# A decoder block on one core: the first loads, the first norm and the constants' addresses are rearranged

## The chip, the core and the metric

The kernel is one program on one of the eight cores of a Trainium2 chip. A core has five engines, each with an instruction stream of its own: TensorE (PE; its weight loads are shown apart as PEld) multiplies matrices, VectorE (DVE), ScalarE (ACT) and GpSimd (POOL) work element by element, and SyncE (SP) issues DMAs. An engine takes its instructions strictly in order; where one waits on a semaphore, all behind it wait too. Data lies in SBUF (128 partitions), results of TensorE in PSUM, everything else in HBM, from which 16 DMA engines load.

The metric is the device time of one execution in microseconds (us); less is better.

## What is computed

One layer of a decoder at 1024 tokens and width 1024, in float32: RMSNorm, an input projection for two kinds of attention with a learned bias by distance, an output projection, a gated feed-forward part, and a final RMSNorm. Cut to what matters here:

```python
h = rmsnorm(x, g_attn[l])
proj = h @ w_in[l]
qa, ka, va, qb, kb, vb = jnp.split(proj, 6, axis=-1)
oa = dilated_attention(qa, ka, va, bias_dil)            # bias from rel_bias by log bucket of distance
lam = (jnp.exp(jnp.sum(lq[0] * lq[1])) - jnp.exp(jnp.sum(lq[2] * lq[3])) + lam_init)
ob = diff_attention(qb, kb, vb, bias_diff, lam, subln_g[l], lam_init)
x = x + jnp.concatenate([oa, ob], axis=-1) @ w_out[l]
h = rmsnorm(x, g_ffn[l])
gate, up = jnp.split(h @ w_gate_up[l], 2, axis=-1)
x = x + (jax.nn.silu(gate) * up) @ w_down[l]
return rmsnorm(x, g_final)
```

with `rmsnorm(x, g) = x * rsqrt(mean(x * x) + eps) * g`.

## The kernel before

All matrix operands are kept as a high part (float32 rounded to the format that TensorE multiplies fast) and a low part (what the rounding left), and each product is the sum of three: high by high, high by low, low by high. The high part is a cast on ScalarE, the low part a subtraction on VectorE or GpSimd.

The first stage, up to about 51 us, is what the change touches. The 1024 tokens are eight tiles of 128. For each tile t the kernel loads `xt_t` (512 KB), squares and sums it on ScalarE (L159), works out `r = (mean + eps) ** -0.5` (`rms_power`, L139 ff.), multiplies by r and by `ga`, the norm's weights, into `hn_a` (two halves on VectorE, L167), transposes that with TensorE against the identity `ident` (`tp_a`, L178, two groups of four), copies the transposes to `hTh` (ScalarE, L181) and what is left to `hTl` (VectorE, L182). Between the tiles TensorE runs `project_v` (L223): the values of two differential heads, 24 matmuls a tile into `vpsd`, against two weight tiles of 512 KB, `w_vd00` and `w_vd01`. Those are loaded as `raw_vd`, cast by ScalarE (L136) and subtracted (L137) by GpSimd for the first and by VectorE for the second. Behind the eight tiles come the query and key weights and projections (`raw_qd`, `raw_kd`, `w_qd`, `ppsqd`).

`rms_power` has two forms. Without `pool` the power is a Ln and an Exp on ScalarE and three small operations on VectorE that refine the result (L148 to L152). With `pool` it is one power on GpSimd (L145). Before, the norm at the start ("a") uses the first form, the norm ahead of the feed-forward part ("f") and the last norm the second.

Beside that, the stage makes the table of biases: `rb` (the learned table) and `hot` (one-hot buckets by distance) are multiplied by TensorE into three PSUM tiles `gps` (L349), VectorE adds `mask` to each and writes `gt` (L350), which is stored as `gtab` (L351) for the attention to read in strips. The lambda of the differential attention comes from `lq` (L364) in two products `lo` on VectorE (L371) and an Exp on ScalarE.

All DMAs are issued from SP's queue, in the order of the code's calls as far as the scheduler keeps it; eight completion semaphores are used in turn, so a DMA is issued only when the one eight places ahead has landed. On the other engines a scheduler orders the instructions from its own estimate of the times, so an edit can move rows that it doesn't name. The tile pools are stacks: those on the left begin behind the constants, those on the right end at the top of SBUF.

The order of the first loads is that of these lines:

```python
    load_x(0)
    nc.sync.dma_start(hot, maps[:N_BUCKETS, :])
    nc.sync.dma_start(rb, rel_bias)
    nc.sync.dma_start(ga, broadcast(g_attn[0], D))
    nc.sync.dma_start(mask, maps[N_BUCKETS:, :])
    nc.sync.dma_start(ident, eye)
```

Of the kernel before, what the change touches and what calls it, by code (L numbers as in the profile page):

```python
# [12 lines left out]
F32 = mybir.dt.float32  # L13
F32R = mybir.dt.float32r
AF = mybir.ActivationFunctionType
ALU = mybir.AluOpType
# [3 lines left out]
P = 128  # L20
S = 1024
D = 1024
# [4 lines left out]
N_HEADS = N_DIL + N_DIFF  # L27
D_FF = 2816
NFF = D_FF // P
N_BUCKETS = 32  # L30
# [4 lines left out]
EPS = 1e-6  # L35
# [5 lines left out]
POOL_POWER = "f"  # L41
# [30 lines left out]
def tile_hybrid_block(  # L72
# [17 lines left out]
    nc = tc.nc  # L90
    mm = nc.tensor.matmul

    cp = ctx.enter_context(tc.tile_pool(name="const", bufs=1))
# [9 lines left out]
    def psum(tag, name):  # L103
        return pp.tile([P, 512], F32, tag=tag, bufs=BANKS[tag], name=name)
# [2 lines left out]
        return ap.partition_broadcast(P) if ap.shape == [n] else ap  # L107


    ident = cp.tile([P, P], F32, name="ident")  # L110
    ones = cp.tile([P, P], F32R, name="ones")
    nhalf = cp.tile([P, 1], F32, name="nhalf")
# [6 lines left out]
    def broadcast(ap1d, n):  # L119
        return bass.AP(tensor=ap1d.tensor, offset=ap1d.offset, ap=[[0, P], [1, n]])  # L120


    def split_weights(src, a, name, tag="w", eng=None, parts=None):

        small = tag == "w"
        pool = wp if small else mapp
        raw = pool.tile([P, 1024], F32, tag="raw" if small else "KL", bufs=1 if small else 2, name=f"raw_{name}")
        nc.sync.dma_start(raw.rearrange("p (a b) -> p a b", a=a), src)
        if parts:
            w = parts  # L130
        elif small:
            w = [pool.tile([P, 1024], F32R, tag=tag, bufs=4, name=f"w_{name}_{i}") for i in "hl"]
        else:
            both = pool.tile([P, 2, 1024], F32R, tag=tag, name=f"w_{name}")
            w = [both[:, i, :] for i in range(2)]
        nc.scalar.copy(w[0], raw)  # L136
        (eng or nc.gpsimd).tensor_tensor(w[1], raw, w[0].bitcast(F32), op=ALU.subtract)  # L137
        return [w_.rearrange("p (a b) -> p a b", a=a) for w_ in w]

    def rms_power(st, eps, pool=False):  # L140

        m, r = st[:, 0:1], st[:, 1:2]
        nc.vector.tensor_scalar(m, m, 1.0 / D, eps, op0=ALU.mult, op1=ALU.add)  # L143
        if pool:
            nc.gpsimd.tensor_tensor(r, m, nhalf, op=ALU.pow)  # L145
            return
        u = st[:, 2:3]
        nc.scalar.activation(r, m, AF.Ln)  # L148
        nc.scalar.activation(r, r, AF.Exp, scale=-0.5)
        nc.vector.scalar_tensor_tensor(u, r, m, r, op0=ALU.mult, op1=ALU.mult)  # L150
        nc.vector.tensor_scalar(u, u, -0.5, 1.5, op0=ALU.mult, op1=ALU.add)
        nc.vector.tensor_tensor(r, r, u, op=ALU.mult)  # L152

    def norm(pool, src, g_b, t, name, hn=None):

        st = pool.tile([P, 3], F32, tag="nst", name=f"nst_{name}{t}")
        if hn is None:
            hn = pool.tile([P, D], F32, tag="hn", bufs=3 if name == "a" else LAG, name=f"hn_{name}{t}")
        nc.scalar.activation(hn, src, AF.Square, accum_out=st[:, 0:1])  # L159
        rms_power(st, EPS, name in POOL_POWER)  # L160
        for half in range(2):
            cols = slice(half * 512, (half + 1) * 512)
            if half and f"{name}{t}" in SHARED:
                nc.scalar.mul(hn[:, cols], src[:, cols], st[:, 1:2])
                nc.gpsimd.tensor_tensor(hn[:, cols], hn[:, cols], g_b[:, cols], op=ALU.mult)
                continue
            nc.vector.scalar_tensor_tensor(  # L167
                hn[:, cols], src[:, cols], st[:, 1:2], g_b[:, cols], op0=ALU.mult, op1=ALU.mult
            )
        return hn  # L170

    def transpose_in(hn, th, tl, t, name):

        for half in range(2):
            ps = psum("T", f"tp_{name}{t}_{half}")
            for i in range(4):
                k = 4 * half + i
                nc.tensor.transpose(ps[:, i * P : (i + 1) * P], hn[:, k * P : (k + 1) * P], ident)  # L178
            pv = ps.rearrange("p (a b) -> p a b", a=4)
            dst = (slice(None), slice(4 * half, 4 * half + 4), slice(t * P, (t + 1) * P))  # L180
            nc.scalar.copy(th[dst], pv)  # L181
            nc.vector.tensor_tensor(tl[dst], pv, th[dst].bitcast(F32), op=ALU.subtract)  # L182
# [14 lines left out]
    gtab = dp.tile([N_HEADS, GLEN], F32, name="gtab")  # L197
# [122 lines left out]
    def load_x(t):  # L320
        xts[t] = sp.tile([P, D], F32, tag="xt", bufs=3, name=f"xt_{t}")
        nc.sync.dma_start(xts[t], x[0, t * P : (t + 1) * P, :])

    rb = sp.tile([N_BUCKETS, N_HEADS], F32, tag="rb", bufs=1, name="rb")
    load_x(0)
    hot = sp.tile([N_BUCKETS, GLEN], F32, tag="hot", bufs=1, name="hot")
    nc.sync.dma_start(hot, maps[:N_BUCKETS, :])
    nc.sync.dma_start(rb, rel_bias)
    mask = sp.tile([N_HEADS, GLEN], F32, tag="mask", bufs=1, name="mask")
    ga = sp.tile([P, D], F32, tag="ga", bufs=1, name="ga")  # L330
    nc.sync.dma_start(ga, broadcast(g_attn[0], D))
    nc.sync.dma_start(mask, maps[N_BUCKETS:, :])
    nc.sync.dma_start(ident, eye)
    ones_f = sp.tile([P, P], F32, tag="ones_f", bufs=1, name="ones_f")
    nc.vector.memset(ones_f, 1.0)
    nc.vector.tensor_copy(ones, ones_f)
    vd = []
    wv = [
        split_weights(
            w_in_v[:, 4 * i : 4 * i + 4, VB : VB + 256], 4, f"vd0{i}", ("QS", "KH")[i], nc.vector if i else None  # L340
        )
        for i in range(2)
    ]

    gt = sp.tile([N_HEADS, GLEN], F32, tag="gt", bufs=1, name="gt")
    for c in range(3):
        ps = psum("S", f"gps_{c}")
        cols = slice(c * 384, (c + 1) * 384)
        mm(ps[:N_HEADS, :384], rb, hot[:, cols], start=True, stop=True)  # L349
        nc.vector.tensor_tensor(gt[:, cols], ps[:N_HEADS, :384], mask[:, cols], op=ALU.add)  # L350
    nc.sync.dma_start(gtab, gt)  # L351
    gen_vd = project_v(VB, False, "d0", vd, wv)
    for t in range(KT):
        if t == 0:
            load_x(1)
        if t + 2 < KT:
            load_x(t + 2)
        transpose_in(norm(sp, xts[t], ga, t, "a"), hTh, hTl, t, "a")
        if t > 0:
            next(gen_vd)  # L360
# [464 lines left out]
    def block_tile(p, up):  # L825
        return mxp.tile([P, 4, 512], F32, tag="mix", name=f"{('gate', 'act')[up]}_{p}")
# [68 lines left out]
    with tc.manual_schedule(engines={mybir.EngineType.PE, mybir.EngineType.Pool}):  # L895
        for i, t in enumerate(TOKENS):
            for n in range(2):
                out_proj_group(mix, wo[n], t, n, "l")
            high = xp.tile([P, D], F32, tag="x1t", name=f"hn_f{t}") if t % 2 else None
            hns[t] = norm(mid, x1[t], gf, t, "f", high)  # L900
            nc.sync.dma_start(x1_d[t], x1[t])
            if 2 <= i < 6:
                flip_low(i - 2)
            if i >= 3 and i < 7:
                split(raw0[0][i - 3], a0[0][i - 3], nc.gpsimd)
        for i in range(4):
            split(raw0[1][i], a0[1][i], nc.gpsimd)
# [29 lines left out]
    for p in range(1, NPAIR):  # L937
        for up in range(2):
# [3 lines left out]
            c = block_tile(p, up)  # L942
# [16 lines left out]
    def next_bank(name):  # L959
        n_ps[0] += 1  # L960
        return psum(CYCLE[n_ps[0] % 8], name)
# [37 lines left out]
    for c0 in range(0, NPAIR - 1, 2):  # L999
# [3 lines left out]
        for i in ORDER:  # L1003
# [14 lines left out]
            for tq in range(4):  # L1018
                ps = next_bank(f"d{c0}_{i}_{tq}")
# [29 lines left out]
    for m, rows in ((0, (2, 3)), (1, (4, 5))):  # L1049
        for tq in range(4):  # L1050
            sl = slice(tq * P, (tq + 1) * P)
            t = 2 * tq + m
            y = xp.tile([P, D], F32, tag="x1t", name=f"y_{t}")
            st = dn.tile([P, 2], F32, tag="fst", bufs=8, name=f"fst_{t}")
            junk = mxp.tile([P, D], F32, tag="mix", name=f"sq_{t}")
            halves = t == KT - 1
            for n, r in enumerate(rows):
                ps = next_bank(f"dl_{t}_{n}")
                i = 0
                for k in range(2):  # L1060
                    a, w = oal[2 * m + k], wl[2 * k + n]
# [3 lines left out]
                cols = slice(n * 512, (n + 1) * 512)  # L1065
# [8 lines left out]
            for n in range(2):  # L1074
                cols = slice(n * 512, (n + 1) * 512)
# [30 lines left out]
```

## Time and profile before

| | |
|---|---|
| median of three runs | 1250.87 us (1249.38 to 1251.2) |
| the profiled execution | 1254.24 us |
| its span, first to last instruction | 1252.5 us |
| mean granted TensorE clock | 0.99 |
| first transposes start | 11.13 us |
| first matmul of the query projection | 51.38 us |

How to read the profile: a row of the timeline has start, duration, engine, source line, operation, the tile written <- the tiles read, the shapes, how many instructions were merged, and in brackets how long the engine was idle just before and what released it. Rows of several instructions run from the first one's start to the last one's end. A row of stretches has, for each engine, the time busy and the number of instructions, then the granted TensorE clock (1.00 is full), the share of time in which the DMA engines were busy, and GB/s. A row of a group has its count, then busy time and the mean duration in ns, then the idle time ahead of it. A row of DMA issues has how many, KB each, and the median time from issue to landing. In the page's slices each digit is a tenth of one of 40 equal slices.

### The profile page before, as it was taken

To read this page: it belongs to the slowest core of one execution; us is meant where nothing else is said; L and a number is where in the kernel's file an instruction comes from. 1 tells how busy PE (TensorE), PEld (TensorE's weight loads), DVE (VectorE), ACT (ScalarE), POOL (GpSimd) and SP (SyncE) were. 2 spreads that over 40 slices of the span, in tenths; PEclk is the share of its full clock that TensorE was granted. 3 is DMA by queue.
4 is the path that set the end of the run, shared out by engine and by line. 5 is a ranking of instruction groups with operands and counts; after the bars stand their busy time and mean duration, and the time that the engine had idled before them with its cause. 6 is when DMAs were issued, how large, how long until landed. Compare 5 with 4: busy or idle time off the path is not lost. (4 is left out here: it accounts for less than half of the span.)

```text
span 1252.5 us, 18470 instructions
## 1 busy us (share of the span) xinstructions
PE 1219.6 (97%) x6318; PEld 1040.9 (83%) x6318; DVE 785.4 (63%) x1667; ACT 576.4 (46%) x1300; POOL 737.3 (59%) x664
## 2 busy tenths in 40 slices
PE   6999999999999999998999999999999999999996
PEld 5989989988998888876788888888888887888885
DVE  6548688876766587858554455554545535655597
ACT  5346567665765565535433443434343433222214
POOL 2024344354443443426936797889878786956676
PEclk8999999999999999998999999999999999999999
DMA  6232233132213383252232345333544369966633
GB/s 217 67 89 71 62 98 89 42 93 87 83 51 108 118 307 132 85 173 104 84 121 88 145 169 184 135 120 133 185 168 175 129 244 372 403 230 253 220 126 134
DMA packets 99613, 184.63 MB, mean 147 GB/s; under 512 B 6920, under 2 KB 58376, under 8 KB 99520
## 3 DMA queue, kind: packets, MB, share of 16 engines
q1 hardware_dynamic: 99520, 183.46, 41.9%
q8 instruction: 50, 0.82, 0.3%
q14 instruction: 43, 0.35, 0.1%
HBM read 119.41 MB, written 55.63 MB: 140 GB/s over the span
## 5 line engine op out<-in xcount | busy, mean ns | idle before, releaser
L1024 PE MATMUL d<-wd,oa 128*128 128x512 f32 x840 | 192.9, 391 | 2.8 <-DMA oa<-act_d 2.6
L1024 PEld LDWEIGHTS d<-wd,oa 128*128 128x128 f32 x840 | 158.5, 189 | 36.9 <-ACT acc L1027 3.0
L1029 DVE TENSOR_TENSOR acc<-d,acc 128x512 f32<-128x512 f32 x128 | 86.5, 687 | 62.7 <-PE d L1024 56.6
L547 POOL TENSOR_SCALAR t_a<-t_a,st_a 128x384 f32<-128x384 f32 (+2 forms) x96 | 55.3, 586 | 104.7 <-DVE st_a L443 71.7
L691 ACT CAST wd<-raw_d 128x512 fp32r<-128x512 f32 x74 | 45.1, 622 | 141.7 <-PE d L1024 95.3
L692 POOL TENSOR_TENSOR wd<-raw_d,wd 128x512 fp32r<-128x512 f32 x54 | 73.0, 1372 | 60.6 <-ACT wd L691 60.6
L692 POOL TENSOR_TENSOR ao<-act,ao 128x512 fp32r<-128x512 f32 x52 | 75.3, 1457 | 42.2 <-ACT ao L691 41.8
L692 POOL TENSOR_TENSOR wu<-raw_u,wu 128x512 fp32r<-128x512 f32 x50 | 69.5, 1408 | 29.8 <-ACT wu L691 17.1
L691 ACT CAST wg<-raw_g 128x512 fp32r<-128x512 f32 x70 | 42.2, 620 | 88.8 <-POOL raw_g L705 43.3
L692 POOL TENSOR_TENSOR wg<-raw_g,wg 128x512 fp32r<-128x512 f32 x50 | 75.0, 1517 | 3.2 <-DVE act L797 2.0
L691 ACT CAST wu<-raw_u 128x512 fp32r<-128x512 f32 x70 | 40.6, 619 | 70.7 <-DMA raw_u<-in_w_gate_up 28.4
L433 ACT ACTIVATE t_d<-t_d,st_d 128x384 f32<-128x384 f32 (+3 forms) x96 | 58.5, 612 | 14.4 <-DVE st_d L420 13.9
L433 ACT ACTIVATE t_a<-t_a,st_a 128x384 f32<-128x384 f32 (+2 forms) x96 | 58.7, 613 | 12.6 <-DVE st_a L420 11.9
L458 ACT CAST ath_a<-tp_a 128x384 fp32r<-128x384 f32 (+2 forms) x96 | 45.1, 478 | 41.4 <-PE tp_a L452 40.3
L752 PE MATMUL pc_g<-h,wg 128*128 128x512 f32 x240 | 59.4, 390 | 0.0
L752 PE MATMUL pa_u<-h,wu 128*128 128x512 f32 x240 | 59.3, 392 | 0.0
L752 PE MATMUL pc_u<-h,wu 128*128 128x512 f32 x240 | 59.2, 389 | 0.0
L752 PE MATMUL pa_g<-h,wg 128*128 128x512 f32 x240 | 58.7, 390 | 0.3 <-ACT gate L778 0.3
L752 PE MATMUL pd_u<-h,wu 128*128 128x512 f32 x240 | 58.5, 389 | 0.0
L752 PE MATMUL pd_g<-h,wg 128*128 128x512 f32 x240 | 57.8, 390 | 0.0
L505 POOL TENSOR_SCALAR t_d<-t_d,st_d 128x384 f32<-128x384 f32 (+3 forms) x48 | 30.1, 637 | 46.8 <-DVE st_d L443 32.2
L691 ACT CAST ao<-act 128x512 fp32r<-128x512 f32 x74 | 42.4, 619 | 32.2 <-DVE act L765 12.2
(275 smaller groups left out, 3577.7 us busy)
## 6 DMA issues: line engine op xcount, KB each, us to landing
act_d<-ao SPq DMA_DIRECT2D x74, 512.0 KB, 3.3
oa<-act_d SPq DMA_DIRECT2D x74, 512.0 KB, 4.9
raw_g<-in_w_gate_up SPq DMA_DIRECT2D x11, 1024.0 KB, 5.7
raw_u<-in_w_gate_up SPq DMA_DIRECT2D x11, 1024.0 KB, 6.2
raw_d<-in_w_down SPq DMA_DIRECT2D x11, 1024.0 KB, 10.1
strip<-gtab SPq DMA_DIRECT2D x12, 512.0 KB, 3.7
xt<-in_x SPq DMA_DIRECT2D x8, 512.0 KB, 5.0
raw_o<-in_w_out SPq DMA_DIRECT2D x8, 512.0 KB, 3.8
```

The costliest lines, as they stand in the source:

```text
L433: nc.scalar.activation(tt[:, :n], tt[:, :n], AF.Exp, bias=st[:, last : last + 1], scale=-1.0, accum_out=st[:, 2 + c : 3 + c],)
L458: nc.scalar.copy(hi, pv)
L505: nc.gpsimd.tensor_scalar(t0[:, :n], t0[:, :n], s0[:, 4:5], 1.0, op0=ALU.mult, op1=ALU.mult)
L547: nc.gpsimd.tensor_scalar(t0[:, :n], t0[:, :n], s0[:, 4:5], 1.0, op0=ALU.mult, op1=ALU.mult)
L691: nc.scalar.copy(dst[:, 0], src)
L692: eng.tensor_tensor(dst[:, 1], src, dst[:, 0].bitcast(F32), op=ALU.subtract)
L752: mm(ps, a[:, l_, k, :], b[:, r_, k, :], start=start and i == 0, stop=i == 11, skip_group_check=not start,)
L1024: mm(ps, a[:, l_, sl], w[:, r_, :], start=n == 0, stop=n == 5)
L1029: v.tensor_tensor(acc[i][:, tq], ps, acc[i][:, tq], op=ALU.add)
```

## The change

Five edits, four of them in the first stage.

- `rb`, `hot`, `ident` and `mask` are loaded from ScalarE's queue, ahead of its first square.
- SP's queue begins with x's first tile, the first weight, `ga`, x's second tile and the second weight.
- The additions of `mask` to `gps` are written as a function that is called ahead of the fourth token tile; the three matmuls keep their place, with three PSUM tiles taken at once.
- The first two token tiles take their power from GpSimd.
- A pad of 128 bytes is put ahead of `ident`. `ident` and `ones` then start at a multiple of 256 bytes (before: 128 past one), and every tile of the left-hand pools moves from a multiple of 256 to 128 past it. The right-hand pools stay.

```diff
+    cp.tile([P, 32], F32, name="const_pad")
     ident = cp.tile([P, P], F32, name="ident")
...
-        rms_power(st, EPS, name in POOL_POWER)
+        rms_power(st, EPS, name in POOL_POWER or name == "a" and t < 2)
...
-    load_x(0)
     hot = sp.tile([N_BUCKETS, GLEN], F32, tag="hot", bufs=1, name="hot")
-    nc.sync.dma_start(hot, maps[:N_BUCKETS, :])
-    nc.sync.dma_start(rb, rel_bias)
     mask = sp.tile([N_HEADS, GLEN], F32, tag="mask", bufs=1, name="mask")
     ga = sp.tile([P, D], F32, tag="ga", bufs=1, name="ga")
-    nc.sync.dma_start(ga, broadcast(g_attn[0], D))
-    nc.sync.dma_start(mask, maps[N_BUCKETS:, :])
-    nc.sync.dma_start(ident, eye)
+    load_x(0)
+    for dst, src in ((rb, rel_bias), (hot, maps[:N_BUCKETS, :]), (ident, eye), (mask, maps[N_BUCKETS:, :])):
+        nc.scalar.dma_start(dst, src)
...
-    wv = [
-        split_weights(
+
+    def first_weights(i):
+        return split_weights(
             w_in_v[:, 4 * i : 4 * i + 4, VB : VB + 256], 4, f"vd0{i}", ("QS", "KH")[i], nc.vector if i else None
         )
-        for i in range(2)
-    ]
+
+    wv = [first_weights(0)]
+    nc.sync.dma_start(ga, broadcast(g_attn[0], D))
+    load_x(1)
+    wv.append(first_weights(1))
...
+    g_ps = [psum("S", f"gps_{c}") for c in range(3)]
     for c in range(3):
-        ps = psum("S", f"gps_{c}")
-        cols = slice(c * 384, (c + 1) * 384)
-        mm(ps[:N_HEADS, :384], rb, hot[:, cols], start=True, stop=True)
-        nc.vector.tensor_tensor(gt[:, cols], ps[:N_HEADS, :384], mask[:, cols], op=ALU.add)
-    nc.sync.dma_start(gtab, gt)
+        mm(g_ps[c][:N_HEADS, :384], rb, hot[:, c * 384 : (c + 1) * 384], start=True, stop=True)
+
+    def bias_tables():
+        for c in range(3):
+            cols = slice(c * 384, (c + 1) * 384)
+            nc.vector.tensor_tensor(gt[:, cols], g_ps[c][:N_HEADS, :384], mask[:, cols], op=ALU.add)
+        nc.sync.dma_start(gtab, gt)
+
     gen_vd = project_v(VB, False, "d0", vd, wv)
     for t in range(KT):
-        if t == 0:
-            load_x(1)
         if t + 2 < KT:
             load_x(t + 2)
+        if t == 3:
+            bias_tables()
         transpose_in(norm(sp, xts[t], ga, t, "a"), hTh, hTl, t, "a")
```

The scheduler makes the following of it. First SP's queue, from the program's start; a name's first number is the token tile or the weight's half, the last one only counts buffers. Before:

```order
L322 DMA xt_0_111<-in_x 128x1024
L327 DMA hot_113<-in_maps 32x1152
L328 DMA rb_110<-in_rel_bias 32x12
L331 DMA ga_117<-in_g_attn 128x1024
L332 DMA mask_116<-in_maps 12x1152
L333 DMA ident_71<-in_eye 128x128
L128 DMA raw_vd00_124<-in_w_in 128x4x256
L128 DMA raw_vd01_129<-in_w_in 128x4x256
L322 DMA xt_1_145<-in_x 128x1024
```

And now, ScalarE's queue behind SP's:

```order
L323 DMA xt_0_115<-in_x 128x1024
L129 DMA raw_vd00_124<-in_w_in 128x4x256
L343 DMA ga_114<-in_g_attn 128x1024
L323 DMA xt_1_130<-in_x 128x1024
L129 DMA raw_vd01_132<-in_w_in 128x4x256
L323 DMA xt_2_144<-in_x 128x1024
L370 DMA lq_586<-in_lambda_qk 128x256
L371 DMA gsub_78<-in_subln_g 128x1
L129 DMA raw_qd0_605<-in_w_in 128x8x128
```

```order
L331 DMA rb_111<-in_rel_bias 32x12
L331 DMA hot_112<-in_maps 32x1152
L331 DMA ident_72<-in_eye 128x128
L331 DMA mask_113<-in_maps 12x1152
L160 ACTIVATE hn_a0_147,nst_a0_146<-xt_0_115 128x1024
L137 CAST w_vd00_126<-raw_vd00_124 128x1024
L160 ACTIVATE hn_a1_170,nst_a1_169<-xt_1_130 128x1024
L137 CAST w_vd01_134<-raw_vd01_132 128x1024
L182 CAST hTh_89<-tp_a0_0_153 128x4x128
```

The first weight stands ahead of `ga` and x's second tile ahead of the second weight; on ScalarE the second tile's square has moved ahead of the second weight's cast, and both are ahead of the first tile's copies.

VectorE, from its first norm on (`nst` holds mean and r, `lo` and `lst` are the lambda's products). Before:

```order
L350 TENSOR_TENSOR gt_134<-gps_0_135,mask_116 12x384
L151 TENSOR_SCALAR nst_a0_149<-nst_a0_149 128x1
L152 TENSOR_TENSOR nst_a0_149<-nst_a0_149 128x1
L167 SCALAR_TENSOR_TENSOR hn_a0_150<-xt_0_111,nst_a0_149,ga_117 128x512 x2
L350 TENSOR_TENSOR gt_134<-gps_1_138,mask_116 12x384
L350 TENSOR_TENSOR gt_134<-gps_2_141,mask_116 12x384
L137 TENSOR_TENSOR w_vd01_131<-raw_vd01_129,w_vd01_131 128x1024
L182 TENSOR_TENSOR hTl_89<-tp_a0_0_160,hTh_88 128x4x128
L182 TENSOR_TENSOR hTl_89<-tp_a0_1_167,hTh_88 128x4x128
```

And now:

```order
L168 SCALAR_TENSOR_TENSOR hn_a0_147<-xt_0_115,nst_a0_146,ga_114 128x512 x2
L355 TENSOR_TENSOR gt_137<-gps_0_138,mask_113 12x384
L355 TENSOR_TENSOR gt_137<-gps_1_139,mask_113 12x384
L355 TENSOR_TENSOR gt_137<-gps_2_140,mask_113 12x384
L144 TENSOR_SCALAR nst_a1_169<-nst_a1_169 128x1
L168 SCALAR_TENSOR_TENSOR hn_a1_170<-xt_1_130,nst_a1_169,ga_114 128x512 x2
L138 TENSOR_TENSOR w_vd01_134<-raw_vd01_132,w_vd01_134 128x1024
L183 TENSOR_TENSOR hTl_90<-tp_a0_0_153,hTh_89 128x4x128
L377 ISA lo_0_591,lst_590<-lq_586 128x64
L377 ISA lst_590 128x1
```

Four more small rows of the lambda follow (`gsub`, `lo_1`, `lst`), and then the other low half of tile 0. The table's sums stand together behind the first tile's product, and the second tile's product has moved from behind the low parts of tile 0 to ahead of the second weight's subtraction.

TensorE, from the projection of tile 0's last terms on. Before:

```order
L223 MATMUL vpsd0_0_203<-w_vd01_131,hTh_88 128x256 x4
L178 MATMUL tp_a1_0_187<-ident_71,hn_a1_177 128x128 x4
L178 MATMUL tp_a1_1_194<-ident_71,hn_a1_177 128x128 x4
L223 MATMUL vpsd0_1_259<-w_vd00_126,hTh_88 128x256 x2
L178 MATMUL tp_a2_0_245<-ident_71,hn_a2_235 128x128 x4
L223 MATMUL vpsd0_1_259<-w_vd00_126,hTl_89 128x256
```

And now (`vpsd0_0` is tile 0's product, and these are its last 16 matmuls and what stands between them):

```order
L179 MATMUL tp_a1_0_176<-ident_72,hn_a1_170 128x128 x4
L224 MATMUL vpsd0_0_192<-w_vd00_126,hTl_90 128x256 x4
L179 MATMUL tp_a1_1_183<-ident_72,hn_a1_170 128x128 x4
L224 MATMUL vpsd0_0_192<-w_vd01_134,hTl_90 128x256 x4
L224 MATMUL vpsd0_0_192<-w_vd00_126,hTh_89 128x256 x4
L224 MATMUL vpsd0_0_192<-w_vd01_134,hTh_89 128x256 x4
L224 MATMUL vpsd0_1_248<-w_vd00_126,hTh_89 128x256 x2
```

Tile 1's transposes have moved into tile 0's product, and tile 2's, which stood inside tile 1's, now stand behind it. On GpSimd the two powers stand one ahead of and one behind the first weight's subtraction. Behind this stage TensorE's and SP's rows are as before; in the second norm, between 560 and 600 us, the scheduler swapped a few rows on VectorE, ScalarE and GpSimd.

## The prediction

> **What bounds the kernel now.** I read the page first, for the engine that is never free and for the slices in which it is.
>
> ```profile
> span 1252.5 us, 18470 instructions
> PE 1219.6 (97%) x6318; PEld 1040.9 (83%) x6318; DVE 785.4 (63%) x1667; ACT 576.4 (46%) x1300; POOL 737.3 (59%) x664
> PE   6999999999999999998999999999999999999996
> PEclk8999999999999999998999999999999999999999
> ```
>
> TensorE is busy 97% of the span; the 33 us in which it is not lie mostly in the first and the last of the 40 slices (31 us each). Every part of the change but the pad lies in the first. So the second view is that stage in stretches:
>
> ```profile
> core 0: us, PE busy (x) PEld busy (x) DVE busy (x) ACT busy (x) POOL busy (x), PEclk, DMA share, GB/s
> 0.00:11.10 11.10, 3.99 (x6) 0.66 (x6) 2.44 (x11) 3.35 (x6) 0.19 (x4) 1.00 0.79 250
> 15.56:18.97 3.41, 3.16 (x15) 3.16 (x16) 3.21 (x18) 2.17 (x8) 0.54 (x1) 1.00 0.12 47
> 18.97:22.38 3.41, 1.47 (x11) 1.02 (x10) 3.38 (x4) 1.27 (x3) 1.81 (x1) 1.00 0.02 1
> 22.38:29.20 6.82, 6.15 (x28) 5.93 (x29) 5.49 (x14) 5.20 (x15) 1.55 (x1) 0.50 0.75 240
> 29.20:51.40 22.20, 22.20 (x191) 22.19 (x191) 17.41 (x46) 11.63 (x34) 0.84 (x1) 1.00 0.35 111
> ```
>
> Until 11.1 us TensorE has only the bias table. From 18.97 to 22.38 it works 1.47 of 3.41 us, and in the 6.8 us after that its granted clock is 0.50. From 29.2 us it is full to the stage's end, the first matmul of the next stage:
>
> ```profile
> 11.13 1.94 PE L178 MATMUL tp_a<-ident,hn_a 128*128 128x128 f32 x8 [1.24 <-DVE hn_a L167]
> 13.48 2.08 PE L223 MATMUL vpsd<-w_vd,hTh 128*128 128x256 f32 x8 [0.41 <-ACT hTh L181]
> 17.68 1.69 PE L223 MATMUL vpsd<-w_vd,hTh 128*128 128x256 f32 x8
> 21.48 0.63 PE L178 MATMUL tp_a<-ident,hn_a 128*128 128x128 f32 x4 [1.68 <-DVE nst_a L152]
> 23.05 0.79 PE L223 MATMUL vpsd<-w_vd,hTh 128*128 128x256 f32 x2 [0.93 <-ACT hTh L181]
> 51.38 0.40 PE L250 MATMUL ppsqd<-hTh,w_qd_h 128*128 128x512 f32 x1
> ```
>
> So the measure is the start of token tile 1's projection, 23.05 us: what stands behind it on TensorE (168 projections, 48 transposes) is the same before and after, and what it gains is kept through the full stages behind, unless TensorE waits anew. What holds it back is on ScalarE, VectorE and GpSimd:
>
> ```profile
> 5.07 1.06 ACT L159 ACTIVATE hn_a<-xt 128x1024 f32<-128x1024 f32 x1 [3.07 <-DMA xt<-in_x]
> 10.59 1.05 ACT L136 CAST w_vd<-raw_vd 128x1024 fp32r<-128x1024 f32 x1 [3.72 <-DMA raw_vd<-in_w_in]
> 11.90 1.05 ACT L136 CAST w_vd<-raw_vd 128x1024 fp32r<-128x1024 f32 x1 [0.26 <-DMA raw_vd<-in_w_in]
> 12.85 1.06 ACT L181 CAST hTh<-tp_a 128x512 fp32r<-128x512 f32 x2
> 9.45 0.55 DVE L350 TENSOR_TENSOR gt<-gps,mask 12x384 f32<-12x384 f32 x1 [2.32 <-DMA mask<-in_maps]
> 10.28 1.42 DVE L167 SCALAR_TENSOR_TENSOR hn_a<-xt,nst_a,ga 128x512 f32<-128x512 f32 x2
> 12.98 2.18 DVE L137 TENSOR_TENSOR w_vd<-raw_vd,w_vd 128x1024 fp32r<-128x1024 f32 x1 [0.36 <-ACT w_vd L136]
> 15.08 1.28 DVE L182 TENSOR_TENSOR hTl<-tp_a,hTh 128x512 fp32r<-128x512 f32 x2
> 17.79 3.55 DVE L167 SCALAR_TENSOR_TENSOR hn_a<-xt,nst_a,ga 128x512 f32<-128x512 f32 x2
> 21.44 1.41 DVE L167 SCALAR_TENSOR_TENSOR hn_a<-xt,nst_a,ga 128x512 f32<-128x512 f32 x2
> 11.72 2.35 POOL L137 TENSOR_TENSOR w_vd<-raw_vd,w_vd 128x1024 fp32r<-128x1024 f32 x1 [11.29 <-ACT w_vd L136]
> 18.43 2.35 POOL L137 TENSOR_TENSOR w_qd_l<-raw_qd,w_qd_h 128x1024 fp32r<-128x1024 f32 x1 [4.36 <-ACT w_qd_h L136]
> ```
>
> Two things are to be seen. The first transposes are done by about 13 us, but their copies (12.85) stand behind the second weight's cast (11.90). And a VectorE operation that reads two SBUF tiles stops while GpSimd subtracts: token 1's pair takes 3.55 us, token 2's 1.41; its second half ends 0.5 us behind GpSimd's 18.43 + 2.35 = 20.78. The weight's subtract, 2.18 us, ends 15.16, 1.09 us after GpSimd's at 14.07: held for 1.09 of it.
>
> **Loads.** Issue to landing, and the small ones:
>
> ```profile
> ga<-in_g_attn SPq DMA_DIRECT2D x1, 512.0 KB, 7.0
> 2.09 0.42 SPq L331 DMA_DIRECT2D ga<-in_g_attn  x1
> 5.91 3.99 PE L349 MATMUL gps<-hot,rb 32*12 32x384 f32 x6 [5.91 <-DMA rb<-in_rel_bias]
> 3.40:6.80 3.40, 0.90 (x2) 0.26 (x3) 0.15 (x1) 1.48 (x4) 0.00 (x0) 1.00 0.76 235
> hot<-in_maps SPq DMA_DIRECT2D x1, 144.0 KB, 4.4
> ```
>
> The two weights land 11.90 - 10.59 = 1.31 us apart, the pace of 512 KB. ga landed at 2.09 + 7.0 = 9.09, 3.2 us behind rb (5.91), with the engines 76% busy: 2.4 us of transfer (bounds 1.31 and 3.2). The four small loads, 264 KB, are 0.67 us at that pace whichever queue issues them. Now xt0 lands at 5.07, the first weight at 5.07 + 1.31 + 0.67 = 7.05, ga at 9.45, xt1 at 10.76, the second weight at 12.07 (it was 11.90), xt2 at 13.4, lq and gsub at 13.7, the query weight at 15.0. Putting the weights ahead of ga is paid back by x's second tile ahead of the second weight: it gains nothing (bounds 10.3 and 12.9). If the small loads took nothing from the big ones, the second weight would land at 11.4. [...] ScalarE's four issues, at SP's 0.42 us, fill a wait of 3.07 us and cost nothing; without that wait they would cost 1.7.
>
> **The engines, step by step.** GpSimd's power costs 0.55 us in the last stage, and takes from VectorE three small operations a token and from ScalarE two:
>
> ```profile
> 1247.53 0.55 POOL L145 TENSOR_TENSOR fst<-fst,nhalf 128x1 f32<-128x1 f32 x1 [0.35 <-DVE fst L143]
> L150 DVE SCALAR_TENSOR_TENSOR nst_a<-nst_a 128x1 f32<-128x1 f32 x8 | 3.3, 410 | 0.5 <-ACT nst_a L149 0.5
> L148 ACT ACTIVATE nst_a<-nst_a 128x1 f32<-128x1 f32 x8 | 1.7, 207 | 0.7 <-DVE nst_a L143 0.7
> ```
>
> - Token 0: squares end 6.25, power 7.0; ga is there at 9.45, but GpSimd subtracts from the first weight's cast (7.05 + 1.05 = 8.1) to 10.45 and holds the pair: 10.45 to 11.9 (it was 10.28).
> - The three table sums stand right behind it, though written for the fourth tile: 1.5 us (0.5 each), to 13.4. Their 2.32 us wait for the mask is gone, but it kept nobody: hn_a waited for ga.
> - Token 1: mean 13.5, power 14.1, pair to 15.5 (it was 21.3: six us earlier). The weight's subtract, not held, 1.09: 16.6. The first half of token 0's low part 0.64: 17.25.
> - ScalarE: square of token 1 10.76 to 12.0; second weight 12.07 to 13.1; token 0's copies to 14.2 (it was 13.9); square of token 2 to 15.4; query weight to 16.45. So GpSimd subtracts from 16.45 to 18.8.
> - VectorE's next is lo, the lambda product, which reads two SBUF tiles. **I take it as held** until 18.8: then 0.5 us of small work and the other low half, to 19.9 (it was 16.36).
> - TensorE needs that for the last 12 matmuls of token 0: at half clock 0.21 each (8 in 1.69, above), 2.5 us: **22.4**, against 23.05, so 0.65 earlier. ScalarE's copy of token 1 (behind the lambda's Exp 19.5, the square of token 3 20.7 and one Ln) ends at 21.5 and keeps nobody.
>
> Given back: token 2's transposes stood inside token 1's projection and now stand behind it, so token 2's projection waits for copy and low part, 0.57 + 0.64, less the second four transposes (0.6) and two matmuls: 0.4 us (0 to 0.9). Sum: -0.65 + 0.4 = **-0.25 us**. The small operations that VectorE no longer does lie beside that wait and are in the times above.
>
> Whether lo is held is not in the trace: the bounds are 0 and 2.35 us, and the nearest rows, pair and weight, were held. [...]
>
> **The pad** sets the identity and the ones at 256 bytes, and moves all tiles of the left-hand pools from 0 to 128 past such a boundary. The trace has no such tile under full load; its nearest rows are xt (64 past), whose loads ran at the pace above, and the transposes' operand hn_a (128 past). I take 0. Should it cost DMA time, the price is bounded by TensorE's later waits for DMAs, doubled: 2.6 + 1.4 us; a gain can't exceed them either.
>
> ```profile
> PE d L1024 <- DMA oa<-act_d: 2.6, 1, 2.6
> PE op L628 <- DMA mixh<-mixh_d: 1.4, 1, 1.4
> PE tp_b L856 <- DVE h L859: 2.6, 2, 1.8
> ```
>
> The scheduler also swaps a few rows of the second norm (ScalarE copies a transpose ahead of token 1's square). That can move the last wait by -1 to +1.1 us (0.58 copy and 0.5 of queue); I take 0.
>
> **Rivals.**
> - **A, the hold is missed.** If the query weight lands 0.8 us later, or lo is not held, lo runs at 17.25, the low half ends at 18.4 and TensorE, done with the transposes at 18.95, starts token 1 at 21.4: -1.65 + 0.4 = -1.25. A denser TensorE may then have its full clock at 25.8 rather than 29.2: 3.4 us at half clock is 1.7 more. Together -2.95: 1247.9 us. For it: 0.8 us decides. Against: every row held so far.
> - **B, slower: the clock.** Token 3's pair may be held by the next GpSimd subtract, and TensorE then idles. One stretch with 1.47 of 3.41 us of work was followed by 6.82 us at 0.50; if that happens once more behind 29.2, where TensorE is full, it loses half of 6.82: 3.4 - 0.25 = +3.15: 1254.0 us. It decides once some 1.5 us of a 3.4 us stretch are idle. Against it: before, full from 23 us on. [...]
> - **C, the pad is felt**: up to 4.0 us either way, 1254.6 at worst.
> - **The change doesn't do what it says**: for the table sums it doesn't (row above); that is in the sum.
>
> **How the numbers follow.** The profiled execution took 1254.24 us, 1.74 more than its span and 3.37 over the median of the three runs, 1250.87; the shift is worked out inside it and applied to the median: 1250.87 - 0.25 = **1250.6**. Chances: forecast 0.55, A 0.27, B 0.13, C 0.05. Its own range is 1248.5 to 1252.5 (landing and give-back bounds, the second norm). The range reaches A's 1247.9 with a further 1.1 and B: 1246.8 to 1254.0. A measurement here tells 0.2%, 2.5 us, from no change. Faster by that: two thirds of A, 0.18, and 0.07 of C and the forecast's tail: 0.25. Slower: 0.11 of B and 0.05 of the rest: 0.16. Within: 0.59.
>
> **What would show it.** In the profile after: the second weight's cast near 12; token 0's copies near 13; the pair of token 1 near 14; GpSimd's query subtract before lo, and the second low half of token 0 near 19.9 (A: near 18.4); token 1's projection near 22.4; the next stage's first matmul within 2 us of 51.4. I am wrong if that stage starts as foreseen and the end does not follow, or if any later line with a left-hand tile changes its time.

## The result, and the profile after

| | before | after |
|---|---|---|
| median | 1250.55 us (1249.38 to 1251.2) | 1262.72 us (1259.57 to 1263.21) |
| ratio, 95% interval | | 1.009 (1.0076 to 1.0103) |
| profiled execution | 1254.24 us | 1263.21 us |
| its span | 1252.5 us | 1261.4 us |

The change makes the kernel 0.9% slower, about 12 us. The forecast was 1250.6 us with a range of 1246.8 to 1254.0, so it missed by 12.1 us, some five times the 0.2% that a measurement tells apart. Further down, one execution of the kernel with the pad alone, 1515.61 us at a granted clock of 0.753, is left out of that kernel's ratio. The page after, the rows that were shown of before:

```profile
span 1261.4 us, 18460 instructions
PE 1228.3 (97%) x6318; PEld 1038.8 (82%) x6318; DVE 782.4 (62%) x1661; ACT 576.0 (46%) x1296; POOL 739.6 (59%) x666
PE   6999999999999999998999999999999999999997
PEclk9999999999999999999999999999999999999999
```

TensorE's busy time grew from 1219.6 to 1228.3 us at the same 6318 instructions, by 8.7 of the 8.9 us that the span grew. (Both are single executions, and the one of before was 3.7 us above its median.) It is as full as before (the slices are the same but for the last), and its clock is no lower (in the mean 0.995 against 0.990). So the time went neither into waits nor into the clock: the matmuls themselves take longer. The stretches in which TensorE is never free show that without any chain of waits; the number in brackets behind the first busy time counts matmuls. Before, then after (700 to 1000 us is gate and up, 1100 to 1200 the down projection):

```profile
700.00:1000.00 300.00, 300.00 (x1322) 247.22 (x1321) 154.76 (x189) 118.88 (x212) 250.65 (x179) 1.00 0.42 150
1100.00:1200.00 100.00, 100.00 (x443) 82.84 (x442) 60.27 (x89) 23.55 (x38) 56.50 (x46) 1.00 0.61 222
```

```profile
700.00:1000.00 300.00, 300.00 (x1305) 245.19 (x1305) 147.73 (x185) 117.25 (x207) 251.63 (x180) 1.00 0.41 146
1100.00:1200.00 100.00, 100.00 (x433) 80.74 (x432) 55.36 (x83) 22.38 (x36) 62.28 (x50) 1.00 0.65 234
```

300 us hold 1322 matmuls of 512 columns before (226.9 ns each) and 1305 after (229.9); in the down projection 100 us hold 443 (225.7) and 433 (230.9). Nothing in these stretches was edited or moved to another place in TensorE's order. Only the addresses are other ones. A closer look at gate and up, TensorE's rows in order of time, before:

```profile
894.79 2.88 PE L752 MATMUL pa_u<-h,wu 128*128 128x512 f32 x12
897.51 0.62 PE L752 MATMUL pb_u<-h,wu 128*128 128x512 f32 x2
897.96 1.98 PE L752 MATMUL pc_u<-h,wu 128*128 128x512 f32 x8
899.78 2.43 PE L752 MATMUL pb_u<-h,wu 128*128 128x512 f32 x10
902.04 1.07 PE L752 MATMUL pc_u<-h,wu 128*128 128x512 f32 x4
902.95 2.88 PE L752 MATMUL pd_u<-h,wu 128*128 128x512 f32 x12
```

and the same 48 matmuls after:

```profile
899.31 2.88 PE L758 MATMUL pa_u<-h,wu 128*128 128x512 f32 x12
902.03 0.62 PE L758 MATMUL pb_u<-h,wu 128*128 128x512 f32 x2
902.49 2.02 PE L758 MATMUL pc_u<-h,wu 128*128 128x512 f32 x8
904.35 2.44 PE L758 MATMUL pb_u<-h,wu 128*128 128x512 f32 x10
906.62 1.10 PE L758 MATMUL pc_u<-h,wu 128*128 128x512 f32 x4
907.56 2.89 PE L758 MATMUL pd_u<-h,wu 128*128 128x512 f32 x12
```

Divide the distance from one row's start to the next one's by the row's count. Before, every row has 225 to 228 ns a matmul (the next row starts at 905.67). After, `pa_u` has (902.03 - 899.31) / 12 = 226.7, `pb_u` 227.0 (the ten) and `pd_u` still 226.7 (the next row starts at 910.28), but `pc_u` (904.35 - 902.49) / 8 = 232.5 and 235 (its four). What sets `pc_u` apart in this trace is its weight tile's place. In a product the weight tile `wu` is the stationary operand and `h` the moving one, 512 columns of it. With the pad all `h` lie 128 bytes past a multiple of 256; the weights of `pa_u`, `pb_u` and `pd_u` here lie in the left-hand pool, also 128 past, and that of `pc_u` in a right-hand one, at a multiple of 256. Before, all of them lay at a multiple. (The tiles of the first stage's pool move by 128 bytes too, but from other places: `xt` from 64 past a multiple of 256 to 192, `hn_a` from 128 past one to a multiple. No matmul of 512 columns reads them.)

The same was done for all matmuls of 512 columns that are followed by another one, with the tiles' addresses in the two programs: the time from start to start, grouped by the distances past a multiple of 256 of the moving rows being read and of the stationary tile being loaded for the next one (after, `pc_u`'s first load starts at 902.26, its first matmul at 902.49). Means, in ns, of starts up to 262 ns apart, so without waits:

| moving / stationary | before | after |
|---|---|---|
| gate and up | 0/0: 227.2 (1824) | 128/0: 232.7 (860); 128/128: 228.0 (978) |
| attention's and the output projections, scores | 0/0: 228.8 (1065) | 0/128: 232.4 (675); 128/0: 232.3 (324); 128/128: 232.4 (73) |
| down | 0/0: 226.8 (925) | 0/128: 231.5 (441); 128/0: 231.1 (24); 0/0: 232.4 (23); 128/128: 231.9 (441) |

In gate and up the pairs in equal places are as fast as before but for 0.8 ns. Elsewhere they are not: in attention (73) and in the down projection (441 and 23) they take as long as the unequal ones beside which they stand, singly or in threes; the last section comes back to it.

In the same way, transposes of 128 columns took 109 ns (median) in both traces, matmuls of 256 columns 119.0 and 118.7. So the loss was looked for in the matmuls of 512 columns, of which there are 4088.

### The profile page after: what moved, and what is told of

Same layout as the page of the kernel before. It is cut to its first block, busy times and chain, and to the rows that moved or that the text cites. A ratio compares the mean times of both kernels' runs of the same rounds, so it can differ in the third digit from the quotient of the medians.

```text
span 1261.4 us, 18460 instructions
## 1 busy us (share of the span) xinstructions
PE 1228.3 (97%) x6318; PEld 1038.8 (82%) x6318; DVE 782.4 (62%) x1661; ACT 576.0 (46%) x1296; POOL 739.6 (59%) x666
## 5 line engine op out<-in xcount | busy, mean ns | idle before, releaser
L1030 PE MATMUL d<-wd,oa 128*128 128x512 f32 x840 | 195.7, 394 | 3.1 <-DMA oa<-act_d 3.1
```

The source lines that it names most:

```text
L1030: mm(ps, a[:, l_, sl], w[:, r_, :], start=n == 0, stop=n == 5)
```

## The experiments

Theory P: the pad is the loss, since a matmul of 512 columns takes longer where its moving and its stationary operand lie at different distances from a multiple of 256 bytes. Rivals, by the letters of the expectations (other ones than the prediction's): the start's new order or the clock (S); tiles at 128 are slow by themselves, through any engine or transfer (A); the constants' place (C).

**The pad away, the rest of the change kept.**

```diff
-    cp.tile([P, 32], F32, name="const_pad")
```

> The changed kernel without const_pad: everything else of the change stays, identity and ones go back to 128 past a multiple of 256 bytes and every tile of the left-hand pools back to a multiple of 256. Theory P (the pad is the loss: the matmul of 512 columns takes longer where its moving rows and its stationary tile lie at different distances from a multiple of 256 bytes, about 232 ns instead of 227 from one matmul start to the next): the loss goes, 1247 to 1251 us, and the stretches 700 to 1000 us again hold 441 or 442 matmuls per 100 us. Rival S (the loss comes from the order at the start, GpSimd's power or the clock there): stays at 1259 to 1263 us, 436 matmuls per 100 us.

1249.27 us, ratio to before 0.9987 (0.9977 to 0.9998). The stretch between 700 and 1000 us:

```profile
700.00:1000.00 300.00, 300.00 (x1322) 247.25 (x1321) 157.60 (x191) 118.56 (x212) 251.03 (x179) 1.00 0.42 151
```

The matmuls are back at 1322, and the loss is gone. TensorE's rows are cut at the end of the window that was asked for, so their counts and lengths are not compared, only their starts. As this kernel and the changed one have the same order on every engine, the first matmuls of the query projection (`ppsqd`), of the up projection (`pa_u`), of the down projection (`d`) and of its last part (`dl`) tell where the pad costs. Without the pad:

```profile
51.02 0.40 PE L250 MATMUL ppsqd<-hTh,w_qd_h 128*128 128x512 f32 x1
598.56 2.89 PE L757 MATMUL pa_u<-h,ops 128*128 128x512 f32 x12
1015.84 3.79 PE L1029 MATMUL d<-wd,oa 128*128 128x512 f32 x16
1216.35 18.98 PE L1068 MATMUL dl<-wd,oa 128*128 128x512 f32 x83
```

and with it, the changed kernel:

```profile
52.64 0.39 PE L251 MATMUL ppsqd<-hTh,w_qd_h 128*128 128x512 f32 x1
604.17 2.89 PE L758 MATMUL pa_u<-h,ops 128*128 128x512 f32 x12
1026.27 3.87 PE L1030 MATMUL d<-wd,oa 128*128 128x512 f32 x16
1230.39 4.79 PE L1069 MATMUL dl<-wd,oa 128*128 128x512 f32 x20
```

From `pa_u` to `d` 422.10 against 417.28 us, 4.8 more; from `d` to `dl` 204.12 against 200.51, 3.6 more; up to `pa_u` 5.6 more (604.17 against 598.56), of which the start has 1.6 (52.64 against 51.02). No stage carries the loss alone.

**The pad alone, put into the kernel before.**

```diff
+    cp.tile([P, 32], F32, name="const_pad")
     ident = cp.tile([P, P], F32, name="ident")
```

> The kernel before with const_pad alone, no other part of the change. Theory P: 1260 to 1264 us, 436 matmuls per 100 us between 700 and 1000 us. Rival S: 1250 to 1251 us, 441 or 442 per 100 us.

1263.06 us, 1.0111 (1.0092 to 1.0129); 1306 matmuls between 700 and 1000 us. All engines have the order of the kernel before. By the intervals the pad alone costs as much as the whole change. S falls.

**Both sides at 128.**

```diff
-    ep.tile([P, 56], F32, name="end_pad")
+    ep.tile([P, 88], F32, name="end_pad")
```

> The changed kernel with end_pad 32 floats longer too (88 for 56), so that the right-hand pools also lie 128 bytes past a multiple of 256, and every one of the 4088 matmuls of 512 columns has both operands at 128. Theory P in the form that the difference of the two operands decides: 227 ns again, 1247 to 1251 us. Rival A (a tile at 128 past a multiple of 256 is itself slower, by a matmul, an engine or a transfer, whatever the other lies at): no faster than the changed kernel, 1262 to 1268 us.

1249.0 us, 0.9991 (0.9978 to 1.0003):

```profile
700.00:1000.00 300.00, 300.00 (x1322) 247.37 (x1321) 156.79 (x190) 117.10 (x208) 251.06 (x180) 1.00 0.44 157
```

Here const_pad is still in, and every one of the 4088 matmuls has both operands at 128 past a multiple; they take 227 ns. Rival A falls: it is not the odd place that costs but two different ones. The order of every engine is that of the changed kernel; only the right-hand tiles have moved.

**The constants at a multiple of 256, the pools too.**

```diff
     nlam = cp.tile([P, 1], F32, name="nlam")
+    cp.tile([P, 32], F32, name="const_tail")
```

> The changed kernel with 32 floats more behind the constants: identity and ones stay at a multiple of 256, as the change has them, and the left-hand pools lie at a multiple of 256 again, as before. Theory P: as without the pad, 1247 to 1251 us, and within 0.1% of e1, since transposes took 109 ns from start to start at both places of the identity. Rival C (the constants' own place costs or gains): differs from e1 by more than 1 us; if their place were the loss, 1260 to 1263 us.

1249.41 us, 0.9982 (0.9972 to 0.9992), against 0.9987 without any pad: the constants' place is worth nothing that these runs tell. This rival C falls. This is also the lowest ratio of all versions; its interval overlaps that of the kernel without the pad.

**Other distances.** The kernel before with 64, 16, 48 or 8 floats for the pad's 32:

```diff
+    cp.tile([P, 64], F32, name="const_pad")
     ident = cp.tile([P, P], F32, name="ident")
```

> The kernel before with a pad of 64 floats (256 bytes) ahead of the constants: everything moves as far again as with const_pad, but keeps its distance from a multiple of 256; the left-hand tiles come to a multiple of 512 and the right-hand ones stay at 256 past one. Theory P with a period of 256 bytes: within 0.2% of the kernel before, 441 or 442 matmuls per 100 us between 700 and 1000 us. Rival M (the period is 512 bytes or more, or any shift of the pools against each other costs): 1260 to 1264 us and 436 per 100 us.

> The kernel before with a pad of 16 floats (64 bytes) ahead of the constants: the left-hand tiles lie 64 bytes past a multiple of 256, the right-hand ones at it; 2484 of the 4088 matmuls of 512 columns then have operands at different distances. Theory P, any difference costs alike: 1260 to 1264 us. Rival H (the cost grows with the difference, or only 128 bytes cost): 1251 to 1257 us.

> The kernel before with a pad of 48 floats (192 bytes) ahead of the constants. In e6, with 64 bytes, the matmuls that began where moving rows lay 64 past the stationary tile's place took 229 ns from start to start, those where they lay 64 short of it 233 ns. Theory D (what counts is moving minus stationary, modulo 256: 0, 64, 128, 192 cost about 0, 2, 5 and 6 ns): the two groups change places, gate and up with moving rows at 192 and stationary tile at 0 take 232 to 234 ns, attention's projections with 0 against 192 take 228.5 to 230; in all 1258 to 1262 us. Rival E (the nearer distance counts, 192 as 64): the groups stay as in e6, 229 in gate and up, 1256.5 to 1259 us.

> The kernel before with a pad of 8 floats (32 bytes) ahead of the constants. Theory D: moving rows 32 past the stationary tile's place cost 0 to 2 ns a matmul, 32 short of it (224) 5 to 7 ns: 1253 to 1258 us. Rival E: both groups cost 0 to 2 ns, 1251 to 1254 us.

| pad, bytes | median, us | ratio, 95% interval | ns, gate and up, moving/stationary | ns, attention |
|---|---|---|---|---|
| 0 | 1250.55 | 1 | 0/0: 227.2 | 0/0: 228.8 |
| 32 | 1261.95 | 1.0080 (1.0068 to 1.0093) | 32/0: 233.4 | 0/32: 232.9 |
| 64 | 1257.8 | 1.0052 (1.0034 to 1.0069) | 64/0: 228.9 | 0/64: 233.3 |
| 128 | 1263.06 | 1.0111 (1.0092 to 1.0129) | 128/0: 232.7 | 0/128: 232.4 |
| 192 | 1259.3 | 1.0063 (1.0051 to 1.0075) | 192/0: 233.2 | 0/192: 230.3 |
| 256 | 1251.4 | 1.0000 (0.9987 to 1.0013) | 0/0: 227.2 | 0/0: 228.9 |

With 256 bytes nothing is lost, though all left-hand tiles moved against the right-hand ones by that much: the period is 256 (of 512 it would have cost), and a shift by itself costs nothing. For 64 the loss was neither that of 128 nor small: 1257.8 us lies between the two ranges that had been written, a little over H's bound, so both missed. The cheap group was the one with moving rows 64 past the stationary tile. The expectation for 192, that the groups change places, held (gate and up 233.2, attention 230.3, both near what was written), and E falls. But 32 bytes refuted both: 1261.95 us, where D had at most 1258. Against the 227.2 and 228.8 ns of equal places, moving minus stationary, modulo 256, costs 1.5 to 1.7 ns a matmul at 64 and 3.6 to 6.2 at 32, 128, 192 and 224. There is no rule here but that 0 is free; why 64 is cheaper, and what it is in the chip that makes two different places collide, stays open.

**Only the moving rows of gate and up.** The kernel before with a pad in the pool of `h`, `ops0` and `wo_l1`; all engines' orders stay:

```diff
     h2p = h2_cm.__enter__()
+    h2p.tile([P, 32], F32, name="h2_pad")
```

> The kernel before with 32 floats (128 bytes) ahead in the pool of h, ops0 and wo_l1 alone: the constants, the weights, attention's tiles and the down stage's stay at their places, while the moving rows of gate and up come to 128 against stationary tiles at 0 in 1728 matmuls of 512 columns. Theory P: the loss lies in gate and up alone, 1728 by 5.2 to 5.5 ns, 9.0 to 9.5 us: 1259 to 1262 us, about 430 matmuls per 100 us between 700 and 1000 us, and the down stage from its first to its last group as long as before. Rival W (the weights', transfers' or constants' places carry the loss, not the operands of a matmul against each other): 1250 to 1252 us.

1256.74 us, 1.0041 (1.003 to 1.0053): less than P had written. The stage itself came out as written. TensorE's first matmuls of the parts, its full stretch, and the wait of the down projection (in all, times, the longest):

```profile
598.48 2.89 PE L753 MATMUL pa_u<-h,ops 128*128 128x512 f32 x12
1025.61 3.80 PE L1025 MATMUL d<-wd,oa 128*128 128x512 f32 x16
1223.36 11.95 PE L1064 MATMUL dl<-wd,oa 128*128 128x512 f32 x52
```

```profile
700.00:1000.00 300.00, 300.00 (x1288) 241.34 (x1287) 151.49 (x185) 116.00 (x204) 244.88 (x176) 1.00 0.39 143
```

```profile
PE d L1025 <- DMA oa<-act_d: 1.0, 2, 0.7
```

From `pa_u` to `d` 427.13 us. In the kernel with the 256-byte pad, where all distances are as before:

```profile
600.16 2.89 PE L753 MATMUL pa_u<-h,ops 128*128 128x512 f32 x12
1017.56 3.79 PE L1025 MATMUL d<-wd,oa 128*128 128x512 f32 x16
1218.15 17.16 PE L1064 MATMUL dl<-wd,oa 128*128 128x512 f32 x75
```

```profile
PE d L1025 <- DMA oa<-act_d: 3.7, 3, 2.6
```

That is 417.40 us. The stage lost 9.7 us, 1288 matmuls in 300 us (232.9 ns). W falls. But from `d` to `dl` it is 197.75 against 200.59 us: 2.8 came back, and the down projection waited 1.0 us instead of 3.7 for its operand's transfers, 2.7 less. Against the trace of the kernel before, 200.82 us with a wait of 2.6, it is 3.1 with 1.6 of them in that wait. So the expectation that the down stage would be as long as before was wrong: a loss ahead of a wait for a transfer was partly paid by that wait, how far differs between these single traces. That leaves 6.9 us; the two executions differ by 5.2 (spans 1254.8 and 1249.6). The other 1.7 lie ahead of `pa_u` (598.48 against 600.16), where the mean granted clock between 580 and 601 us was 1.00 here and 0.92 there.

**The start's two parts alone.** The loads, weights and sums without GpSimd's power, and that power alone in the kernel before:

```diff
-        rms_power(st, EPS, name in POOL_POWER or name == "a" and t < 2)
+        rms_power(st, EPS, name in POOL_POWER)
```

> The changed kernel without const_pad and with ScalarE's power for both first tiles, as before: the loads, the weights and the bias sums alone are changed. If what the change gains besides the pad lies in the order of the loads and sums: 0.998 to 0.9995 of the kernel before, as e1 was (0.9987). If it lies in GpSimd's power: within 0.1% of the kernel before.

> The kernel before with GpSimd's power for the first two tiles and nothing else. If the gain besides the pad lies in the order of the loads and sums: within 0.1% of the kernel before. If it lies in GpSimd's power: 0.998 to 0.9995 of it. The prediction's own sum has no gain from it alone.

1249.81 us, 0.9990 (0.9979 to 1.0002), and 1250.0 us, 0.9991 (0.9978 to 1.0003). Neither is told from no change, and neither expectation is refuted; together with the pad away they gave 0.9987, 1.6 us. How that gain divides stays open.

## Why the prediction was wrong

**The failed step is the pad.** The prediction said: "I take 0. Should it cost DMA time, the price is bounded by TensorE's later waits for DMAs, doubled", 4.0 us. The pad cost 1.11% when measured alone, 13.9 us (11.5 to 16.1 by the interval). It cost TensorE's time, not DMA time: its busy time grew by 8.7 of the 8.9 us, and the down projection's wait for transfers was 3.1 us in the changed kernel and 2.7 in the one without the pad. The bound was drawn round the wrong mechanism. Its nearest rows were a load's pace (`xt`) and transposes with `hn_a`, and neither is a matmul of 512 columns. In `hn_a`'s transposes both operands lay 128 past a multiple, and the transposes of later stages, with 128 against 0, took the same 109 ns in the trace of before: transposes couldn't show this cost. What was missing was a price per matmul: the trace of before had all 4088 matmuls of 512 columns at 0/0, so no row of it showed another case, and any price per matmul of the size of a few ns times 4088 was open. By the pairs of the table above, 5.5 ns by 860 and 0.8 by 978 in gate and up, 4.9 by some 930 in down and 3.6 by 1072 ahead of them, 13.9 us in all; the traces with and without the pad differ by 1261.4 - 1247.9 = 13.5 us. 13.9 less the 1.6 us that the rest of the change gains is 12.3, and the change measured 12.2. The prediction did write the sentence that would show it wrong ("if any later line with a left-hand tile changes its time"), and that is what happened; the prediction's own rival C, with 0.05, named the place but not the mechanism or the size.

**The start.** Its steps can be followed in the changed kernel, rows by engine:

```profile
12.25 1.04 ACT L137 CAST w_vd<-raw_vd 128x1024 fp32r<-128x1024 f32 x1 [0.27 <-DMA raw_vd<-in_w_in]
13.20 1.06 ACT L182 CAST hTh<-tp_a 128x512 fp32r<-128x512 f32 x2
13.73 1.42 DVE L168 SCALAR_TENSOR_TENSOR hn_a<-xt,nst_a,ga 128x512 f32<-128x512 f32 x2 [0.67 <-POOL nst_a L146]
16.94 2.36 POOL L138 TENSOR_TENSOR w_qd_l<-raw_qd,w_qd_h 128x1024 fp32r<-128x1024 f32 x1 [3.25 <-ACT w_qd_h L137]
17.00 2.38 DVE L377 CUSTOM_DVE_ANT_0 lo<-lq 128x64 f32<-128x64 f32 x1
19.31 0.68 DVE L183 TENSOR_TENSOR hTl<-tp_a,hTh 128x512 fp32r<-128x512 f32 x1
20.04 1.12 PE L179 MATMUL tp_a<-ident,hn_a 128*128 128x128 f32 x4 [1.14 <-DVE nst_a L144]
21.81 2.10 PE L224 MATMUL vpsd<-w_vd,hTh 128*128 128x256 f32 x10
```

- Loads: the second weight's cast at 12.25 (foreseen 12.07). Right. The trace of before has one queue alone, so that the small loads take 0.67 us from the big ones from another queue too was the author's estimate. Here ScalarE waits for x's first tile until 4.61 and for the first weight until 6.94, 2.33 us apart, where the sum had 1.31 + 0.67.
- Token 1's pair ends 15.15 (15.5), token 0's copies 14.26 (14.2). Right.
- The hold of `lo`: the first product (16.79) starts ahead of GpSimd, the second takes 2.38 us, to just behind GpSimd's end at 19.30, and the other low half ends 19.99 (19.9). Right. No row of before has `lo` beside GpSimd; the hold was the author's estimate from the pair and the weight. Without the pad and in the fourth experiment the first product started behind GpSimd (17.21 behind 16.31, 16.34 behind 15.51) and, like the second one here, ended 0.08 us behind GpSimd's end.
- Token 1's projection: eight matmuls behind 21.81, at about 23.5 (foreseen 22.4). Wrong by 1.1 us: the second four transposes of tile 1 were taken to be done at 18.95, but started at 20.04, just behind the second low half (the row's bracket names the small row of VectorE behind that half). They write the PSUM bank that this half still reads, and the program waits for it there. The step left out a bank that is used in turn.
- What was given back: token 2's projection waited 1.64 us for its copy, where the sum had 0.4 (0 to 0.9). Wrong. The key weight's subtract on GpSimd held the last half of token 3's product (the four halves of tokens 2 and 3 took 4.90 us). VectorE's low part of `Vd` stood behind that half, and on ScalarE a row ahead of token 2's copy waited 1.32 us for `Vd`:

```profile
25.00 2.39 POOL L138 TENSOR_TENSOR w_kd_l<-raw_kd,w_kd_h 128x1024 fp32r<-128x1024 f32 x1 [5.71 <-ACT w_kd_h L137]
23.04 4.90 DVE L168 SCALAR_TENSOR_TENSOR hn_a<-xt,nst_a,ga 128x512 f32<-128x512 f32 x4
28.18 0.27 ACT L228 CAST Vd<-vpsd 128x128 fp32r<-128x128 f32 x1 [1.32 <-DVE Vd L229]
29.07 0.50 PE L224 MATMUL vpsd<-w_vd,hTh 128*128 128x256 f32 x2 [1.64 <-ACT hTh L182]
```

- Even so token 2's projection started 0.7 us earlier than before (29.07 against 29.79). The next stage began at 52.64, 1.3 us later than the 51.38 of before instead of 0.25 earlier, mostly by a stretch at half the granted clock that is shown below.

With both sides at 128 the program is the same up to addresses, and this fell the other way:

```profile
17.04 0.21 DVE L377 CUSTOM_DVE_ANT_0 lo<-lq 128x64 f32<-128x64 f32 x1
17.05 2.43 POOL L138 TENSOR_TENSOR w_qd_l<-raw_qd,w_qd_h 128x1024 fp32r<-128x1024 f32 x1 [3.33 <-ACT w_qd_h L137]
18.73 1.05 PE L179 MATMUL tp_a<-ident,hn_a 128*128 128x128 f32 x4
48.38 0.40 PE L251 MATMUL ppsqd<-hTh,w_qd_h 128*128 128x512 f32 x1
```

`lo` starts 0.01 us ahead of GpSimd and takes 0.21 us, and the next stage begins at 48.38. That is the prediction's rival A, whose -2.95 from 51.38 is 48.43. The sum fits better than its steps, which is partly luck: token 1's projection began at about 21.9 (21.4 in A), and no stretch behind it had a granted clock under 1.00, where A had left one of 3.4 us. Nor was it `lo` alone. Here the four halves of tokens 2 and 3 took 2.74 us, from 21.59, as the last one had begun ahead of the key weight's subtract (24.30). Token 2's projection waited 0.41 us, what the sum had:

```profile
26.22 0.50 PE L224 MATMUL vpsd<-w_vd,hTh 128*128 128x256 f32 x2 [0.41 <-ACT hTh L182]
```

In the kernel of the fourth experiment `lo` was held (1.77 us), the four halves were not (2.74), and the next stage began at 48.97; in the one without the pad both were (1.78 and 4.87), and it began at 51.02. In these four traces it is this second hold that goes with the late starts.

**Its rival B** named that hold, for token 3's pair, and was seen in the changed kernel at half its price, in these two stretches one behind the other:

```profile
26.89:30.31 3.42, 1.55 (x12) 1.11 (x11) 3.06 (x9) 2.13 (x7) 0.50 (x1) 1.00 0.45 117
30.31:33.72 3.41, 3.41 (x19) 3.41 (x18) 2.78 (x8) 1.28 (x5) 0.00 (x0) 0.50 0.95 258
```

1.55 of 3.42 us of work, and then a granted clock of 0.50 for 3.41 us in which TensorE is full, 1.7 us lost. The 1.5 us of idle time that the prediction gave as deciding was the author's estimate beside one row, with 1.94 us. Laid end to end through the traces of before and after, from the first record of the clock on, eight stretches of 3.41 us at a granted clock of 1.00 were followed by one at 0.50: they had 1.81 to 3.41 us of idle time, this one 1.87. All others at 1.00 had at most 1.47 us. All these are single executions; over many the change without its pad gains 1.6 us (0.3 to 2.9 by its interval, which just reaches the 0.25 of the sum), and its 1249.27 us lie inside the forecast's own 1248.5 to 1252.5. The table sums stood behind the first tile's product as foreseen (11.53 to 13.00). What the second norm's swapped rows did, no run tells apart.

## What to carry to other kernels

A pad is an edit of every matmul whose operands lie in two different pools. Before costing it at nothing, list the two operands' distances from a multiple of 256 bytes, multiply the count of the pairs that would differ by a few ns (shown here for 512 columns alone), and see whether the product can be measured. If one group of tiles has to move, move the other by as much (88 floats for 56 gave the whole loss back), or fill up behind the small constants, as the fourth experiment does. And count the matmuls in stretches where TensorE is full, before and after: it tells a slower rate from a new wait in one row.

## What the runs showed of the hardware

- A matmul of 512 columns follows the one before by 227 ns (228.8 in the mean in attention's part) where moving and stationary operand lie at the same distance from a multiple of 256 bytes, and by 231 to 234 where they don't (229 to 230 with the moving one 64 past). The equal pairs need a longer row to get there: in the down projection, where three with 128/128 alternate with three with 0/128, both groups took 231.5 to 231.9, and in gate and up the first 128/128 behind an unequal pair took 232.7 in the mean, the fourth 230.2, those from the eleventh on 226.7. Transposes of 128 columns showed none of it, and matmuls of 256 lost nothing: 119.0 at 0/0, 118.7 at 128/0, and less, 117.0 and 115.7, at 32/0 and 192/0.
- Less than 0.1 us decides whether a product is held: `lo` at 17.00, behind GpSimd's 16.94, took 2.38 us, and at 17.04, ahead of its 17.05, 0.21. Between the two traces the next stage's first matmul differs by 4.3 us, with the second hold and the stretch at half the clock in it.
- The clock in a row isn't always the rate. In the changed kernel's start, matmuls of 256 columns followed each other by 213 ns up to 23.5 us and by 120 behind it. The trace has no record of the clock ahead of 23.48 us (that of before, ahead of 18.97), and a row shows 1.00 there too; the prediction's "half clock" for its 0.21 us is such a rate, and its own row there has 1.00. And in the kernel of the fourth experiment the row for 700 to 1000 us has a granted clock of 0.95 and yet 1321 matmuls:

```profile
700.00:1000.00 300.00, 300.00 (x1321) 247.24 (x1320) 156.63 (x190) 116.76 (x208) 250.78 (x180) 0.95 0.43 155
```
